# First down pair of each quarter starting with another product, and the weights' sums made in place

## The chip, the cores and the metric

The kernel runs on one core of a Trainium2 chip. The metric is the device time of one execution in microseconds. Before the change it is 960.91 us, the median of three runs (959.47 to 961.05). A profile is one more execution, taken with the hardware profiler.

## The reference, cut to what matters

The program is one decoder block for one sequence of 512 tokens with 1024 channels, in float32: a Mamba-2 mixer and a pooling mixer merged by gates, then an MLP, then a final norm. The change lies in the MLP:

```python
h = rmsnorm(x, norm_mlp_w[i]) * (1.0 + scale_f) + shift_f
x = x + gate_f * (jnp.square(jax.nn.relu(h @ w_up[i])) @ w_down[i])
```

`w_up` is 1024 x 4096 and `w_down` 4096 x 1024.

## The kernel before, in words

**Float32 products.** TensorE is fed numbers of a shorter float format (`fp32r`). A float32 operand is therefore split in two: the high half is a cast on ScalarE (L837, in `two`), the low half is the difference on VectorE, called DVE in the profile (L839). A product is three matmuls: high times high, high times low, low times high. In the plain products these are the lines L156, L157 and L158 (`mm3`), with 512 columns each; in the pairs, all three are L875 (`product`), with 256 columns.

**Quarters.** The 4096 hidden channels are worked on in four quarters q. Within a quarter come the up products (1024 hidden channels, held as eight tiles `us[0]` to `us[7]`, each squared after the ReLU and split), then the down products, which add that quarter's share to x.

**Pairs.** Most of this goes in pairs of 128-wide output tiles, each by seven half-size products of a Strassen-Winograd scheme in place of eight: a 2 x 2 block matrix of weights A11, A12, A21, A22 against a 2 x 2 block matrix of activations B. The weights come with sums formed on the way. `Pair.fetch` loads three tiles: `ya` (1024 wide), `yb` (1024 wide) and `y4` (512 wide). SP issues the three loads (L888, L889, L891), and GpSimd's queue (POOL) then adds further weights onto `ya` and `yb` while loading them (L892, L894). In a pair that is called *led* (the first down pair of each quarter) the second of these adds is made on DVE instead (L911).

From `ya` come the operands S1 and A11 as one split; from the sums z come S2 and S4 as one split; from `yb` come S3 and A12 as one split; `y4` gives A22. The sums are two additions on DVE, 512 wide: the first half of z is the sum of the two halves of `ya` (L908), the second half is the first half of z plus the second half of `yb` (L919). z has a tile of its own.

**The order of a pair.** `run_jobs` writes out the order. Pair after pair it is: A11 times B11 (`first`), the last two products of the pair before (`close` S4, `finish` A22), the preparation of the next pair's `ya` (`prepare`), S2 and then A12 (`middle`), the next pair's sums and its S2/S4 split (`prepare_more`), the next pair's S1 (`open`), S3 (`third`), and then the next pair's S3/A12 and A22 splits (`prepare_rest`). Each product is 4 x 3 = 12 matmuls, so a pair is 84.

The first down pair of a quarter follows a plain down product (`down_plain`, two output tiles), because it needs sums of `us` that are only ready late. Its own preparation is written around that product: `prepare` and `prepare_more` before it, `prepare_rest` behind it. The pair itself then begins with `lead`: A12 times B21 into `c11`, A11 times B11 into `ac`; ScalarE copies `ac` out (L946), DVE adds the copy onto `c11` (L947). It is followed by `open`.

**Slots.** Tiles are given out by `Slots`, first in, first out. RL has four slots for `ya` and `yb`, so two pairs' weights are in flight; a tile that a fetch writes waits until the last reader of its previous content is through. HL has nine slots of 1024 for the high and low halves of split weights; one more tile of that size holds z. The units of `down_plain` take four HL slots, a led pair's S1/A11 and S2/S4 take four.

**What orders the instructions.** The kernel doesn't write the queues out directly: a planner at build time puts the instructions of each engine in a fixed order, from their order in the program, a higher priority where the code says so, and its own estimates of durations. `tc.issue_after(x)` keeps an instruction behind x on x's engine. `mids` holds the DVE additions of the `middle` and `third` products; the sums and some low halves are kept behind the latest of them.

Of the kernel before, what the change touches and what calls it, by code (L numbers as in the profile page):

```python
# [10 lines left out]
ALU = mybir.AluOpType  # L11

P = 128
T = 512
# [26 lines left out]
H = T // 2  # L41
# [21 lines left out]
def block_kernel(tc, xp, crow, arow, par, adaT, wstart, wz, wx, wpool_in, wgate, wpw, wbs, wbp, wout, wup, wdn, out):  # L63
    nc = tc.nc
    act, dve, pool, pe, sp = nc.scalar, nc.vector, nc.gpsimd, nc.tensor, nc.sync

    with (
# [15 lines left out]
        def D(i, dt, o=0):  # L83

            count[0] += 1
            w = 1024 if i < NRAW else 1088
            return sb.tile([P, w], dt, tag=f"d{i}", name=f"d{i}_{count[0]}", bufs=1)[:, o:o + 1024]

        RAW = Slots(D, NRAW)
        HL = Slots(lambda i, dt: D(NRAW + i, dt), NHL)  # L90
        MT = Slots(lambda i, dt: D(NRAW + NHL + i, dt).rearrange("p (h k) -> p h k", h=HG), 3)
# [44 lines left out]
        def load_unit(src, n=1024, low=None, at=None, cols=1024):  # L136

            at = at or HL
            with tc.high_priority() if urgent[0] else nullcontext():
# [76 lines left out]
        def warm(n):  # L216

            ps = PS.get()
            b = busy[:, :T // 2].bitcast(mybir.dt.bfloat16)
            for _ in range(n):  # L220
                pe.matmul(ps, b[:, :P], b, start=True, stop=True)
            PS.put(ps)
# [3 lines left out]
        with tc.manual_schedule():  # L226
# [3 lines left out]
            mt = [MT.get() for _ in range(3)]  # L230
            xs1 = HL.get()
            xpair = [m.rearrange("p h k -> p (h k)") for m in mt] + [xs1]
# [4 lines left out]
            warm(12)  # L237
            wide = HL.get()
            dve.memset(wide, 0.0)
            act.activation(wide[:1], crow_t, AF.Silu)  # L240
            cps = [PU.get(), PU.get()]
            for i in range(2):
                pe.matmul(cps[i], ones, wide[:, i * T:(i + 1) * T], start=True, stop=True)
            HL.put(wide)
            ps = PU.get()
            sq = [HL.get() for _ in range(4)]

# [217 lines left out]
        def ssd_group(g):  # L465
# [20 lines left out]
            def prepare(c):  # L486
# [28 lines left out]
                return m, xdt, xd  # L515

            ready = [prepare(0)]
            yield
            for c in range(NC):
                cc = slice(c * P, (c + 1) * P)  # L520
                if c < NC - 1:
                    ready.append(prepare(c + 1))
                    yield
# [300 lines left out]
        raws = [SZ.get(), SZ.get()]  # L824
        B0 = NRAW
        RL = Slots(lambda i, dt: D(i, dt), 4)
        Z = Slots(lambda i, dt: D(B0 + 8, dt), 1)
        HL = Slots(lambda i, dt: D(B0 + i if i < 8 else B0 + 9, dt, 48), 9)
        HI0 = Slots(lambda i, dt: D(B0 + 10 + i, dt), 2)
        U = Slots(lambda i, dt: slots("pad", 1, (P, T + 16), first=OTHER[i]).get(dt)[:, :T] if i < 2 else spare[i - 2], 4)  # L830
        spare = [S.get(), S.get()]
# [3 lines left out]
        def two(src, dst, late=None):  # L835

            act.copy(dst[0], src)  # L837
            with tc.issue_after(late.ins) if late else nullcontext():
                dve.tensor_tensor(dst[1], src, dst[0].bitcast(F32), ALU.subtract)  # L839
# [37 lines left out]
        class Pair:  # L877
# [25 lines left out]
            def prepare(self):  # L903
                ya = self.y[0]
                self.a, self.left = {}, {}
                z = Z.get()
                with tc.issue_after(mids[-1].ins) if mids and self.led else nullcontext():
                    dve.tensor_tensor(z[:, :T], ya[:, :T], ya[:, T:], ALU.add)  # L908
                if self.led:
                    yb = self.y[1]  # L910
                    dve.tensor_tensor(yb[:, :T], yb[:, :T], ya[:, T:], ALU.add)  # L911
                self.keep(ya, "S1", "A11")
                RL.put(ya)
                self.z = z

            def prepare_more(self):
                z, yb = self.z, self.y[1]
                with tc.issue_after(mids[-1].ins) if mids else nullcontext():
                    dve.tensor_tensor(z[:, T:], z[:, :T], yb[:, T:], ALU.add)  # L919
                self.keep(z, "S2", "S4")  # L920
                Z.put(z)

            def prepare_rest(self):
                yb = self.y[1]
                self.keep(yb, "S3", "A12")
                RL.put(yb)
                hl = Y4S.get(F32R), Y4S.get(F32R)
                two(self.y4, hl)
                Y4S.put(*hl)
                Y4.put(self.y4)  # L930
                self.a["A22"] = hl
# [7 lines left out]
            def lead(self):  # L939
                self.take()  # L940
                self.ac = AC.get()
                self.mul(self.c11, "A12", "B21", True)
                self.mul(self.ac[:, :H], "A11", "B11", True)
                t = U5.get()
                with tc.high_priority():
                    act.copy(t, self.ac[:, :H])  # L946
                    dve.tensor_tensor(self.c11, self.c11, t, ALU.add)  # L947
                U5.put(t)
# [136 lines left out]
        mids = []  # L1085
# [246 lines left out]
```

## Time and profile before

| | |
|---|---|
| median of three runs | 960.91 us |
| lowest, highest | 959.47, 961.05 us |
| the profiled execution | 958.36 us |
| its span | 956.6 us |
| mean granted TensorE clock | 0.995 |
| PE (TensorE matmul) busy | 940.4 us, 98% |
| PEld (its weight loads) busy | 810.9 us, 85% |
| DVE busy | 721.3 us, 75% |
| ACT (ScalarE) busy | 540.8 us, 57% |
| POOL (GpSimd) busy | 124.3 us, 13% |

The span is the time from the first to the last instruction; the difference to the profiled execution's time lies around it. The MLP's pairs take the last 300 us of the span or so. A group row reads: line, engine, operation, output and inputs by the program's names, shape, count, then busy us, mean ns of one, and the engine's idle time just ahead with what ended it. A timeline row begins with the start and the duration in us from the beginning of the span; the brackets at its end hold the idle time before it and what released it. A row of the windows gives the stretch, its length, the busy us of PE, PEld, DVE, ACT and POOL, the granted clock, the DMA share and GB/s. In a row of the chain stand the start, the length and what the time was spent on.

### The profile page before, as it was taken

Reading aid. Unit: us, or ns where it says so; the run is one execution under the profiler, and the core shown is the slowest. Engines: PE = TensorE matmul, PEld = TensorE weight load, DVE = VectorE, ACT = ScalarE, POOL = GpSimd, SP = SyncE. Lnnn points to the kernel's source line nnn. Section 1 sums busy time; section 2 is a strip of 40 time slices with the busy share of each in tenths; the row PEclk is TensorE's granted clock in tenths of the full one; section 3 lists DMA queues with packets and bytes.
Section 4 is the critical chain, followed back from the end, with each engine's and each line's share of the span. In section 5 each row is a group of like instructions: output and inputs, shape, how many; then the busy total and the mean of one; then the engine's idle time right before and its main releaser. Section 6 shows DMA issues by size and latency. Waiting matters only on the chain.

```text
span 956.6 us, 14343 instructions
## 1 busy us (share of the span) xinstructions
PE 940.4 (98%) x5491; PEld 810.9 (85%) x5491; DVE 721.3 (75%) x1120; ACT 540.8 (57%) x891; POOL 124.3 (13%) x131
## 2 busy tenths in 40 slices
PE   8999999999999999999999999999999999999996
PEld 4877888888888888787888888998999899899986
DVE  7978868566767776987568565698869888977973
ACT  5479976568436642553421343486458547646753
POOL 0102320220312031410000000001111111111000
PEclk9999999999999999999999999999999999999998
DMA  9836343433354343464578464035676676677412
GB/s 362 310 119 181 118 129 98 136 121 97 88 144 122 99 116 96 158 192 156 181 237 287 152 201 151 29 91 126 159 200 152 151 198 147 165 194 169 133 35 88
DMA packets 70503, 145.55 MB, mean 152 GB/s; under 512 B 5473, under 2 KB 30305, under 8 KB 70434
## 3 DMA queue, kind: packets, MB, share of 16 engines
q1 hardware_dynamic: 64672, 134.14, 44.5%
q0 software_dynamic: 5760, 10.49, 7.4%
q8 instruction: 43, 0.70, 0.3%
q14 instruction: 26, 0.21, 0.1%
q10 hardware_dynamic: 2, 0.00, 0.0%
HBM read 142.39 MB, written 2.23 MB: 151 GB/s over the span
## 4 chain that ended last, share of the span: by engine, by line
PE 75%; DVE 12%; DMA 5%; ACT 4%; issue 2%; POOL 0%; SPq 0%; DVEq 0%; POOLq 0%; ACTq 0%
PE ps L875 18%; PE ps L156 16%; PE ps L157 16%; PE ps L158 16%; PE ps L328 4%; DMA d<-wdn 3%; DVE d L839 2%; DVE d L147 1%; PE ps L549 1%; DMA d<-cs_d 1%; DVE s L127 1%; DVE s L839 1%; ACT d L837 1%; PE ps L529 1%; DMA d<-wstart 1%
## 5 line engine op out<-in xcount | busy, mean ns | idle before, releaser
L156 PE MATMUL ps<-s,d 128*128 128x512 f32 (+1 forms) x920 | 350.6, 381 | 1.1 <-ACT s L649 0.6
L157 PE MATMUL ps<-s,d 128*128 128x512 f32 (+1 forms) x920 | 345.9, 376 | 0.2 <-DVE s L127 0.2
L158 PE MATMUL ps<-s,d 128*128 128x512 f32 (+1 forms) x920 | 346.0, 376 | 0.0
L156 PEld LDWEIGHTS ps<-s,d 128*128 128x128 f32 x920 | 172.6, 188 | 35.7 <-issue 2.1
L158 PEld LDWEIGHTS ps<-s,d 128*128 128x128 f32 x920 | 172.8, 188 | 32.4 <-issue 0.2
L157 PEld LDWEIGHTS ps<-s,d 128*128 128x128 f32 x920 | 172.8, 188 | 31.2 <-DVE s L127 0.7
L875 PE MATMUL ps<-s,d 128*128 128x256 f32 x1314 | 162.2, 279 | 2.1 <-DVE d L839 2.0
L875 PEld LDWEIGHTS ps<-s,d 128*128 128x128 f32 x1314 | 156.9, 188 | 4.2 <-DVE d L839 3.8
L147 DVE TENSOR_TENSOR d<-d,d 128x1024 fp32r<-128x1024 f32 x88 | 112.6, 1280 | 63.1 <-ACT d L146 56.6
L146 ACT CAST d<-d 128x1024 fp32r<-128x1024 f32 x88 | 92.0, 1046 | 117.8 <-PE ps L157 77.2
L837 ACT CAST d<-d 128x1024 fp32r<-128x1024 f32 x86 | 89.8, 1048 | 56.9 <-DVE d L919 24.1
L839 DVE TENSOR_TENSOR d<-d,d 128x1024 fp32r<-128x1024 f32 x86 | 104.7, 1221 | 18.9 <-ACT d L837 10.2
L172 DVE CUSTOM_DVE_ANT_0 d<-d,d,par_t 128x1024 f32<-128x1024 f32 x32 | 41.8, 1306 | 27.3 <-DMA d<-adaT 27.1
L892 POOL DMA_DIRECT2D d<-wdn x10 | 8.8, 884 | 307.5 <-DMA d<-wdn 258.7
L328 PE MATMUL ps<-s,d 128*128 128x512 f32 x168 | 41.7, 403 | 1.9 <-ACT s L316 1.9
L499 ACT ACTIVATE d<-d,ncs 128x128 f32<-128x128 f32 x128 | 39.9, 390 | 3.9 <-POOL d L495 3.8
L328 PEld LDWEIGHTS ps<-s,d 128*128 128x128 f32 x168 | 32.5, 194 | 10.0 <-ACT s L316 2.4
L397 DVE SCALAR_TENSOR_TENSOR s<-ps,par_t,s 128x511 f32<-128x511 f32 (+2 forms) x54 | 39.6, 741 | 0.3
L126 ACT CAST s<-s 128x512 fp32r<-128x512 f32 x32 | 19.7, 619 | 31.1 <-POOL s L511 18.7
L495 POOL TENSOR_SCALAR_AFFINE_SELECT d<-d 128x1024 f32<-128x1024 f32 x16 | 18.2, 1137 | 90.8 <-ACT cd L492 37.0
L127 DVE TENSOR_TENSOR s<-s,s 128x512 fp32r<-128x512 f32 x32 | 25.7, 805 | 4.4 <-ACT s L126 4.3
L511 POOL TENSOR_TENSOR s<-s,dec 128x512 f32<-128x512 f32 x12 | 15.8, 1313 | 90.7 <-issue 56.4
(231 smaller groups left out, 1231.6 us busy)
## 6 DMA issues: line engine op xcount, KB each, us to landing
d<-adaT SPq DMA_DIRECT2D x32, 512.0 KB, 4.2
d<-wup SPq DMA_DIRECT2D x32, 512.0 KB, 4.8
d<-wdn SPq DMA_DIRECT2D x32, 512.0 KB, 4.6
d<-wx SPq DMA_DIRECT2D x18, 512.0 KB, 3.6
d<-cs_d SPq DMA_DIRECT2D x16, 512.0 KB, 6.0
d<-wbs SPq DMA_DIRECT2D x16, 512.0 KB, 3.6
d<-wgate SPq DMA_DIRECT2D x16, 512.0 KB, 4.2
d<-wz SPq DMA_DIRECT2D x15, 512.0 KB, 3.6
```

The costliest lines, as they stand in the source:

```text
L146: act.copy(hi[:, :w], r[:, a:a + w])
L147: (low or dve).tensor_tensor(lo[:, :w], r[:, a:a + w], hi[:, :w].bitcast(F32), ALU.subtract)
L156: pe.matmul(ps, whi, xhi[:, t0:t1], start=start, stop=False)
L157: pe.matmul(ps, whi, xlo[:, t0:t1], start=False, stop=False)
L158: pe.matmul(ps, wlo, xhi[:, t0:t1], start=False, stop=stop)
L172: dve.tensor_tensor_reduce(r, r, cbc, 1.0, col("b_ada", j), ALU.mult, ALU.add, mod[:, j:j + 1])
L328: pe.matmul(first[u], w[u][i // 2], h[k][i % 2], start=k == 0 and i == 0, stop=k == 7 and i == 2)
L397: dve.scalar_tensor_tensor(t[:, sh:], ps[:, :T - sh], w(3 - sh), t[:, sh:], ALU.mult, ALU.add)
L499: act.activation(m[:, i, :], m[:, i, :], AF.Exp, bias=ncs[:, c, g * HG + i:g * HG + i + 1])
L837: act.copy(dst[0], src)
L839: dve.tensor_tensor(dst[1], src, dst[0].bitcast(F32), ALU.subtract)
L875: pe.matmul(ps, x, y, start=start and m == 0 and i == 0, stop=m == 3 and i == 2, skip_group_check=True)
```

## The change

Four edits in the pairs of the MLP.

1. `lead`, the beginning of the first down pair of each quarter, makes A11 times B11 first and A12 times B21 second. Before, it was the other way round.
2. The sums have no tile of their own any more. The first is written over the first half of `ya`, after the S1/A11 split has read it; the second over the second half of `ya`. `ya` is given back after the S2/S4 split, not after the S1/A11 split. The first sum of a led pair is no longer kept behind `mids`.
3. The tile that z had becomes the tenth HL slot, for split weights.
4. The S3/A12 split moves from `prepare_rest` to the end of `prepare_more`: ahead of the next pair's S1 and this pair's S3 product in the program, and for a led pair ahead of the plain down product.

```diff
--- before.py
+++ after.py
@@ -824,8 +824,7 @@
         raws = [SZ.get(), SZ.get()]
         B0 = NRAW
         RL = Slots(lambda i, dt: D(i, dt), 4)
-        Z = Slots(lambda i, dt: D(B0 + 8, dt), 1)
-        HL = Slots(lambda i, dt: D(B0 + i if i < 8 else B0 + 9, dt, 48), 9)
+        HL = Slots(lambda i, dt: D(B0 + i, dt, 48), 10)
         HI0 = Slots(lambda i, dt: D(B0 + 10 + i, dt), 2)
         U = Slots(lambda i, dt: slots("pad", 1, (P, T + 16), first=OTHER[i]).get(dt)[:, :T] if i < 2 else spare[i - 2], 4)
         spare = [S.get(), S.get()]
@@ -903,27 +902,22 @@
             def prepare(self):
                 ya = self.y[0]
                 self.a, self.left = {}, {}
-                z = Z.get()
-                with tc.issue_after(mids[-1].ins) if mids and self.led else nullcontext():
-                    dve.tensor_tensor(z[:, :T], ya[:, :T], ya[:, T:], ALU.add)
                 if self.led:
                     yb = self.y[1]
                     dve.tensor_tensor(yb[:, :T], yb[:, :T], ya[:, T:], ALU.add)
                 self.keep(ya, "S1", "A11")
+                dve.tensor_tensor(ya[:, :T], ya[:, :T], ya[:, T:], ALU.add)
+
+            def prepare_more(self):
+                ya, yb = self.y
+                with tc.issue_after(mids[-1].ins) if mids else nullcontext():
+                    dve.tensor_tensor(ya[:, T:], ya[:, :T], yb[:, T:], ALU.add)
+                self.keep(ya, "S2", "S4")
                 RL.put(ya)
-                self.z = z
-
-            def prepare_more(self):
-                z, yb = self.z, self.y[1]
-                with tc.issue_after(mids[-1].ins) if mids else nullcontext():
-                    dve.tensor_tensor(z[:, T:], z[:, :T], yb[:, T:], ALU.add)
-                self.keep(z, "S2", "S4")
-                Z.put(z)
-
-            def prepare_rest(self):
-                yb = self.y[1]
                 self.keep(yb, "S3", "A12")
                 RL.put(yb)
+
+            def prepare_rest(self):
                 hl = Y4S.get(F32R), Y4S.get(F32R)
                 two(self.y4, hl)
                 Y4S.put(*hl)
@@ -939,8 +933,8 @@
             def lead(self):
                 self.take()
                 self.ac = AC.get()
+                self.mul(self.ac[:, :H], "A11", "B11", True)
                 self.mul(self.c11, "A12", "B21", True)
-                self.mul(self.ac[:, :H], "A11", "B11", True)
                 t = U5.get()
                 with tc.high_priority():
                     act.copy(t, self.ac[:, :H])
```

## The prediction

> **What bounds the kernel now.** I read the page first, then the waits of TensorE, then the timeline of the MLP stage engine by engine. Page, parts 1 and 5:
>
> ```profile
> span 956.6 us, 14343 instructions
> ...
> PE 940.4 (98%) x5491; PEld 810.9 (85%) x5491; DVE 721.3 (75%) x1120; ACT 540.8 (57%) x891; POOL 124.3 (13%) x131
> ...
> L875 PE MATMUL ps<-s,d 128*128 128x256 f32 x1314 | 162.2, 279 | 2.1 <-DVE d L839 2.0
> L875 PEld LDWEIGHTS ps<-s,d 128*128 128x128 f32 x1314 | 156.9, 188 | 4.2 <-DVE d L839 3.8
> ```
>
> TensorE is the bound. In the products of the pairs (L875) its only wait that sums to anything is for L839 on DVE, the low half of a split of weights: 2.0 us as idle PE, 3.8 us as idle weight loads. The timeline of the weight loads shows where:
>
> ```profile
> 673.07 2.65 PEld L875 LDWEIGHTS ps<-s,d 128*128 128x128 f32 x22 [0.74 <-DVE d L839]
> 737.20 3.95 PEld L875 LDWEIGHTS ps<-s,d 128*128 128x128 f32 x33 [0.35 <-DVE d L839]
> 754.28 2.65 PEld L875 LDWEIGHTS ps<-s,d 128*128 128x128 f32 x22 [0.60 <-DVE d L839]
> 818.42 3.93 PEld L875 LDWEIGHTS ps<-s,d 128*128 128x128 f32 x34 [0.36 <-DVE d L839]
> 835.25 2.57 PEld L875 LDWEIGHTS ps<-s,d 128*128 128x128 f32 x22 [0.49 <-DVE d L839]
> 897.58 2.54 PEld L875 LDWEIGHTS ps<-s,d 128*128 128x128 f32 x21 [0.94 <-DVE d L839]
> 914.43 2.65 PEld L875 LDWEIGHTS ps<-s,d 128*128 128x128 f32 x22 [0.36 <-DVE d L839]
> ```
>
> Seven waits, 3.84 us together. By the order of the products, 673, 754, 835 and 914 are the first product of the four led pairs, A12 times B21 (0.74 + 0.60 + 0.49 + 0.36 = 2.19 us). The other three, 737, 818 and 898, are A12 times B21 in the last up pair of a quarter, just ahead of the plain down product (`down_plain`, L1180) (0.35 + 0.36 + 0.94 = 1.65 us). All seven wait for the low half of A12. Why it is late in the second quarter, from DVE, ScalarE, the queues and PE:
>
> ```profile
> 726.79 0.34 SPq L888 DMA_DIRECT2D d<-wdn  x1
> 730.65 1.22 DVE L839 TENSOR_TENSOR d<-d,d 128x1024 fp32r<-128x1024 f32 x1
> 734.79 2.35 DVE L839 TENSOR_TENSOR d<-d,d 128x1024 fp32r<-128x1024 f32 x2
> 736.04 1.05 ACT L837 CAST d<-d 128x1024 fp32r<-128x1024 f32 x1 [1.32 <-DMA d<-wdn]
> 737.00 0.62 ACT L1093 ACTIVATE pad<-pad 128x512 f32<-128x512 f32 x1
> 741.37 0.62 ACT L837 CAST d<-pad 128x512 fp32r<-128x512 f32 x1 [0.92 <-DVE pad L844]
> 743.08 0.62 ACT L837 CAST d<-pad 128x512 fp32r<-128x512 f32 x1 [0.81 <-DVE pad L846]
> 744.77 1.22 DVE L839 TENSOR_TENSOR d<-d,d 128x1024 fp32r<-128x1024 f32 x1
> 749.79 1.02 DVE L839 TENSOR_TENSOR s<-s,s 128x512 fp32r<-128x512 f32 x2
> 751.66 0.39 PE L157 MATMUL ps<-s,d 128*128 128x512 f32 x1
> 753.01 1.22 DVE L839 TENSOR_TENSOR d<-d,d 128x1024 fp32r<-128x1024 f32 x1
> ```
>
> The row at 753.01 is A12's low half; it ends at 754.23 and PE resumes at 754.28. DVE has no idle time before it: its place in DVE's order makes it late, and that place comes from the slots. Of nine slots for split weights the down product's two units hold four and the led pair's S1/A11 and S2/S4 four, so the second tile of S3/A12 is one that the first unit gives back at the end of the down product. A11's low half was done at 744.77 + 1.22 = 745.99, more than seven us before its turn. At 734.79 the second of two rows is A12's low half of the last up pair, behind those of the down product's own units.
>
> **The change part by part.** Instruction and DMA counts stay. The sums change their tile:
>
> ```profile
> L908 DVE TENSOR_TENSOR d<-d x22: 678/690/695, 652.8 to 903.5; 128x512 f32<-128x512 f32 x22
> L911 DVE TENSOR_TENSOR d<-d,d x4: 683/684/685, 654.3 to 904.1; 128x512 f32<-128x512 f32 x4
> ```
>
> L911 already sums in place and takes 684 ns against 690 for L908: zero, at most 22 x 6 ns either way.
>
> *A11 first in the led pair.* A11 is split in time in all four quarters if its row keeps its place, and the product is 12 matmuls, half of the 24 that take about 2.65 us at 754.28, so 1.3 to 1.4 us of cover. The longest led wait is 0.74. This edit alone takes the 2.19 us even if the split of A12 doesn't move. The add of L947 needs both products as before.
>
> *Tenth slot and sooner split.* S3/A12 is now taken with S2/S4, before the down product, and ten slots are just enough (4 + 6), so no tile has to come back from the units. In the pairs that follow each other the third operand no longer waits for the product of the one before. This takes the 1.65 us ahead of the down products. What remains is whether DVE has room. Removed: upper bound 3.84; lower bound 2.0, the idle of PE itself from the page; I take 3.5, nearer the upper, since weight loads and matmuls alternate one by one here and a late load is a late product.
>
> *What is late next.* S3/A12's low half (1.22 us) now ranks before the splits of the last activated tile, us[7]. That is the first of the two rows at 749.79 (half of a merged row, some 0.69 us long, so done at 750.48); PE reads it at 751.66: 1.18 us to spare. In the first quarter there is less:
>
> ```profile
> 669.15 1.03 DVE L839 TENSOR_TENSOR s<-s,s 128x512 fp32r<-128x512 f32 x2
> 670.30 0.39 PE L157 MATMUL ps<-s,d 128*128 128x512 f32 x1
> ```
>
> Done at about 669.85, read at 670.30: 0.45 us. Pushed by 1.22: 0.04 us in later quarters and 0.77 in the first; from the latter the first sum of the next pair (L908, 0.69) is to be taken off, since it now stands behind that pair's own split. Bounds 0 and 1.1 us, I take 0.5.
>
> *The first weight tile is held longer.* It was free after the low half of S1/A11; now after that of S2/S4, because the sums live in it. The refill is one SP load and one POOL add, in this order on both queues. Among the up pairs:
>
> ```profile
> 692.88 1.22 DVE L839 TENSOR_TENSOR d<-d,d 128x1024 fp32r<-128x1024 f32 x1
> 694.13 0.34 SPq L888 DMA_DIRECT2D d<-wup  x1
> 699.30 1.23 DVE L839 TENSOR_TENSOR d<-d,d 128x1024 fp32r<-128x1024 f32 x1 [0.24 <-ACT d L837]
> 700.41 0.86 POOL L892 DMA_DIRECT2D d<-wup  x1 [0.38 <-issue]
> 711.29 1.05 ACT L837 CAST d<-d 128x1024 fp32r<-128x1024 f32 x1 [0.98 <-PE ps L875]
> 712.71 0.36 ACT L968 COPY ps<-ps 128x256 f32<-128x256 f32 x1 [0.36 <-PE ps L875]
> 715.34 8.64 PE L875 MATMUL ps<-s,d 128*128 128x256 f32 x72
> ...
> d<-wup POOLq DMA_DIRECT2D x24, 256.0 KB, 4.3
> ```
>
> (The last row is from the page's DMA issues.) The load at 694.13 goes right behind the low half that ends at 694.10. It will go behind the one that ends at 700.53, 6.4 us later. Its tile was whole at about 700.41 + 4.3 + 0.9 = 705.6 (the 0.9 being the issue itself) and cast at 711.29, when a slot came free from PE: 5.7 us of cover. So the cast comes some 0.7 us later, 712.0, and its low half ends by about 714.4. The products of the row at 715.34 are S2 and A12 of the pair before, 24 matmuls at 0.118, and then S1, which reads it at about 718.2: nothing lost, while the loads take no longer. Behind the cast on ScalarE stands L968, whose copy must be out before that S2 at 715.34; it ends at 713.07 and has 2.3 us. The second tile (L889, L894) is freed sooner and costs nothing. Taken as 0, bounds -0.2 and +2 us for the whole stage.
>
> **Sum.** -3.5 + 0.5 + 0 = -3.0 us. The profiled execution took 958.36 (span 956.6 and 1.76 around it), 2.55 below the median 960.91 of the three runs shown. So 955.4 for a run like it, and 957.9 against the median.
>
> **The rivals.**
>
> *The split moves, the wait moves with it.* If both halves of S3/A12 are put ahead of us[7], 1.05 us on ScalarE joins the 1.22: 2.27 - 1.18 = 1.09 us in three quarters and 1.82 in the first, 5.1 us. -3.5 + 5.1 = +1.6, 962.5. For it: DVE is nearly full there.
>
> ```profile
> 720.00:760.00 40.00, 39.57 (x288) 37.10 (x288) 36.03 (x60) 27.92 (x50) 4.33 (x5) 1.00 0.66 164
> ```
>
> 36.03 of 40 us on DVE (fourth number after the colon; PE 39.57). Against: the total doesn't grow and ScalarE, at 27.92, has room for the cast anywhere.
>
> *Slower: a cast that waits for a late tile holds ScalarE.* At 736.04 the cast of the led pair's S1/A11 had already held ScalarE for 1.32 us, waiting for its weights. Their load (726.79) went behind S1/A11 of the up pair before; it will go behind the low half that ends at 730.65 + 1.22 = 731.87, 5.1 us later, so the tile is whole at 741.2. If the cast keeps its place ahead of L1093, the whole chain of us[6] and us[7] starts 5.1 us late. ScalarE's idle rows of 0.92 and 0.81 give back at most 1.7, us[7] has 1.18 to spare: 2.2 to 3.9 us in each of three quarters (the first quarter's led weights come in slots that plain units held). 6.6 to 11.7, say 9; with the -3.5 it is 966.4. It decides from a tile more than 1.2 us behind its place. Against: the written order is made knowing the later load, so the cast should move down, and S1/A11 has over seven us before its use.
> The Trainium skill, "TensorE: Matmul & The Clock Gate", section "Architectural detail: the array is 16× 32×32, not 1× 128×128", speaks for this one: ScalarE's and VectorE's queues are strict FIFO, only TensorE pulls anything forward. The 1.32 us at 736.04, with work right behind it, agrees.
>
> *Half of it.* The planner leaves A12's low half last on DVE. Then the three waits ahead of the down products stay: -2.19, 958.7.
>
> *The pace of PE.* The chain of waits has three long runs of products:
>
> ```profile
> 673.07 50.93 PE ps L875 x430
> ...
> 754.28 50.93 PE ps L875 x430
> ...
> 835.25 57.06 PE ps L875 x501
> ```
>
> 118.4, 118.4 and 113.9 ns a product, the same instructions at the same granted clock (1.00). The pace differs from one restart after a wait to the next, and the change removes the restarts. If the third run falls to the slow pace, 501 x 4.5 ns = 2.3 us are lost: 960.2. If the first two rise, 2 x 430 x 4.5 ns = 3.9 us are won: 954.0. Nothing in the trace says which; the forecast leaves each run its pace.
>
> **How the numbers follow.** Forecast (956.8 to 959.1, from -3.84 with nothing given back to -2.0 with little) 0.48; half 0.12; the wait moves 0.14; pace lost 0.08; pace won 0.06; ScalarE held 0.12. A measurement of this kernel tells about 0.2%, 1.9 us, from no change: faster is below 959.0. Faster: most of the forecast, half of the half, the pace won, 0.55. Slower, above 962.8: ScalarE held and a tail of the moved wait, 0.14. Within: 0.31. The range 954.4 to 962.4 takes in all but the held ScalarE and the edges of the moved wait and the won pace.
>
> **What would show it.** Right: no wait for L839 at the first product of a led pair, nor in the last up pair of a quarter, idle weight loads there below 1 us together; A12's low half before us[7]'s or soon after, and ahead of the sums of u; SP's first load of a pair behind S2/S4. Wrong: new waits of L156 to L158 for an s tile of L839 in the down product (the wait moved); ScalarE idle for several us on a weight load ahead of L1093 (held); the L875 runs at another mean per product (pace).

## The result and the profile after

The changed kernel takes 968.5 us, the median of four runs (967.32 to 972.54). The kernel before, run beside it, takes 960.25. The ratio is 1.0106, with a 95% interval of 1.0085 to 1.0127: 1.1% slower, and outside the predicted range. The profiled execution took 968.73 us, its span is 967.0.

Lines have moved: the cast of a split is now L836 (before L837), the low half L838 (L839), a pair's products L874 (L875), the loads of `ya` and `yb` L887 and L888, the first sum L909, the second L914, the DVE add of a led pair's `yb` L907, the DVE sum of `middle` L967 (L973), the ReLU of the up products L1086 (L1092). From the page of the changed kernel:

```profile
PE 945.4 (98%) x5491; PEld 813.2 (84%) x5491; DVE 719.8 (74%) x1120; ACT 540.3 (56%) x891; POOL 124.7 (13%) x131
...
L874 PE MATMUL ps<-s,d 128*128 128x256 f32 x1314 | 162.3, 279 | 1.2 <-DVE ps L967 1.2
L874 PEld LDWEIGHTS ps<-s,d 128*128 128x128 f32 x1314 | 157.8, 188 | 2.2 <-DVE ps L967 1.7
```

The wait for the low half of A12 is gone from both groups: where 2.0 and 3.8 us stood under L839, the releaser is now L967. The busy times of DVE and ScalarE are the same as before within 1.5 us, so no work was added. The same is seen in the waits of the whole changed kernel (engine, what it works on, what it waited for; us in total, times, longest):

```profile
PE ps L874 <- DVE ps L967: 2.4, 5, 0.9
...
PE ps L156 <- ACT pad L1086: 1.4, 1, 1.4
...
PE ps L156 <- ACT s L836: 1.3, 2, 1.1
...
PE ps L157 <- DVE s L838: 1.0, 3, 0.4
```

None of these four rows is in the view of before. They sum to 6.1 us of idle PE. TensorE now waits for the middle sums of pairs (L967; two of the five waits stand in the last up pair of a quarter, three in down pairs) and, in the plain products (L156, L157), for activated tiles.

What is late ahead of them? The same view between 622 and 945 us, for the weights alone (`wup` and `wdn` are the sources in memory). Changed kernel:

```profile
ACT d L836 <- DMA d<-wup: 13.4, 5, 3.6
ACT d L836 <- DMA d<-wdn: 11.4, 3, 4.3
DVE d L907 <- DMA d<-wdn: 3.2, 2, 2.8
```

Kernel before:

```profile
DVE d L908 <- DMA d<-wdn: 4.6, 1, 4.6
...
ACT d L837 <- DMA d<-wdn: 3.9, 3, 1.5
```

ScalarE's casts of weights stood waiting for loads for 24.8 us, against 3.9 before. How such a wait gets to TensorE shows in the second quarter. ScalarE, changed kernel, with the tile's loads from SP's queue and the products that come too late:

```profile
736.70 1.79 SPq L887 DMA_DIRECT2D d<-wdn  x2
742.29 0.62 ACT L836 CAST s<-pad 128x512 fp32r<-128x512 f32 x1
746.78 1.05 ACT L836 CAST d<-d 128x1024 fp32r<-128x1024 f32 x1 [3.87 <-DMA d<-wdn]
747.74 0.38 ACT L1086 ACTIVATE s<-ps 128x256 f32<-128x256 f32 x1
754.06 1.05 ACT L836 CAST d<-d 128x1024 fp32r<-128x1024 f32 x1 [1.35 <-DVE d L914]
755.02 0.63 ACT L1087 ACTIVATE s<-s 128x512 f32<-128x512 f32 x1
756.52 0.49 PE L156 MATMUL ps<-s,d 128*128 128x512 f32 x1 [0.17 <-ACT s L836]
757.36 0.50 PE L157 MATMUL ps<-s,d 128*128 128x512 f32 x1 [0.35 <-DVE s L838]
```

The row at 746.78 is the cast of the led pair's S1/A11. It held ScalarE for 3.87 us (1.32 before); its load was issued at 736.70 (726.79 before; PE's products around it stand some 3.9 us later as well, so about 6 us of this are the tile's). Behind it stands the ReLU of us[6] (L1086), and then comes us[7]. The cast of S2/S4 (754.06) stands ahead of us[7]'s square as it did before, and waited 1.35 us for the second sum on DVE (0.37 before). The square (755.02) ends at 755.65, and its split comes when TensorE already needs it. The middle sums hang on late tiles too, at least in one case: in the down pair where PE waits at 703.41, DVE's work was held by a cast that had waited 3.47 us for its weights (ScalarE, 697.19).

Not all of the difference of the two profiles is the change's. Counting PE's instructions from the start, the 3000th begins at 617.87 us before and at 620.00 after, ahead of all work that the change touches. The other 8.3 us arise behind it. There PE's waits, taken as what each start-to-start time has above the usual 0.118 or 0.2285 us, sum to 10.5 us against 4.7. The third long run of products has lost its fast pace, some 2.3 us, but others have won it: counted over all pairs, 282 products ran at the fast pace against 581 before, some 1.3 us lost. The last 1.1 us were not taken apart.

### The profile page after: what moved, and what is told of

Its sections match the earlier page's. It is cut to its first block, busy times and chain, and to the rows that moved or that the text cites. A ratio compares the mean times of both kernels' runs of the same rounds, so it can differ in the third digit from the quotient of the medians.

```text
span 967.0 us, 14359 instructions
## 1 busy us (share of the span) xinstructions
PE 945.4 (98%) x5491; PEld 813.2 (84%) x5491; DVE 719.8 (74%) x1120; ACT 540.3 (56%) x891; POOL 124.7 (13%) x131
## 4 chain that ended last, share of the span: by engine, by line
PE 68%; DVE 15%; DMA 7%; ACT 5%; issue 4%; POOL 0%; SPq 0%; DVEq 0%; ACTq 0%; POOLq 0%
PE ps L156 16%; PE ps L157 16%; PE ps L158 16%; PE ps L874 12%; PE ps L328 4%; DMA d<-wdn 4%; DVE d L838 2%; DMA d<-cs_d 2%; DVE d L147 2%; ACT d L836 1%; DVE s L127 1%; PE ps L549 1%; DMA d<-wup 1%; DVE s L838 1%; DVE pad L631 1%
## 5 line engine op out<-in xcount | busy, mean ns | idle before, releaser
L156 PE MATMUL ps<-s,d 128*128 128x512 f32 (+1 forms) x920 | 351.1, 382 | 4.2 <-ACT pad L1086 1.4
L157 PE MATMUL ps<-s,d 128*128 128x512 f32 (+1 forms) x920 | 346.7, 377 | 1.3 <-DVE s L838 1.0
L156 PEld LDWEIGHTS ps<-s,d 128*128 128x128 f32 x920 | 172.6, 188 | 40.7 <-ACT s L836 2.5
L157 PEld LDWEIGHTS ps<-s,d 128*128 128x128 f32 x920 | 172.8, 188 | 33.0 <-DVE s L838 2.0
L874 PE MATMUL ps<-s,d 128*128 128x256 f32 x1314 | 162.3, 279 | 1.2 <-DVE ps L967 1.2
L874 PEld LDWEIGHTS ps<-s,d 128*128 128x128 f32 x1314 | 157.8, 188 | 2.2 <-DVE ps L967 1.7
L836 ACT CAST d<-d 128x1024 fp32r<-128x1024 f32 x86 | 89.6, 1049 | 85.5 <-DVE d L914 26.2
L838 DVE TENSOR_TENSOR d<-d,d 128x1024 fp32r<-128x1024 f32 x86 | 104.7, 1222 | 43.4 <-ACT d L836 37.2
L874 PE MATMUL ps<-sz,d 128*128 128x256 f32 x180 | 26.7, 283 | 1.1 <-DVE ps L967 1.1
```

The lines of the kernel that those rows point to most:

```text
L156: pe.matmul(ps, whi, xhi[:, t0:t1], start=start, stop=False)
L157: pe.matmul(ps, whi, xlo[:, t0:t1], start=False, stop=False)
L874: pe.matmul(ps, x, y, start=start and m == 0 and i == 0, stop=m == 3 and i == 2, skip_group_check=True)
```

## The experiments

In the expectations, "traced" means written in the program; the planner makes the queues from it.

### The order of the led pair alone

```
 (kernel before)
             def lead(self):
-                self.mul(self.c11, "A12", "B21", True)
                 self.mul(self.ac[:, :H], "A11", "B11", True)
+                self.mul(self.c11, "A12", "B21", True)
```

> The kernel before with one edit: each led pair's product of block 11 (A11) is traced ahead of A12's, nothing else. Theory (the first weight tile, held longer, is what costs the 8 us): this edit doesn't touch that tile, so the four waits of led pairs for A12's low half (2.19 us in all in the profile of before) go, the three of the last up pairs (1.65 us) stay, and the time is 957.5 to 958.5. Rival (the led pair's new order itself is harmful, as A11's unit is needed one product, about 1.4 us, sooner): new waits for A11's low half stand where the old ones stood, and the time is 960 to 964.

Measured: 955.5 us beside 959.81, ratio 0.9957 (0.9943 to 0.9971). Faster, and by more than the 2.19 us of the waits; the interval of the gain is 2.8 to 5.5 us. The rival falls. In the profile the chain of waits shows that pace helped here:

```profile
673.95 63.63 PE ps L875 x538
...
754.25 31.30 PE ps L875 x276
...
834.08 57.02 PE ps L875 x503
```

118.3, 113.4 and 113.4 ns a product (length over count): the second of these ran at the fast pace too. Counted from start to start, 1087 of the pairs' products ran at it, against 581 in the first profile of the kernel before; at 4.5 ns each this is 2.3 us, as much as the two profiled executions differ (956.14 and 958.36). PE's waits in the pairs fell by only 0.9 us, since the waits of the last up pairs for A12 grew. So how much of the 4.3 us belongs to the order is not settled.

### The sums in place alone, and the tile held alone

```
 (kernel before, first experiment)
-        z = Z.get(); first sum: z[:, :T] = ya[:, :T] + ya[:, T:]
         self.keep(ya, "S1", "A11")
-        RL.put(ya)
+        first sum: ya[:, :T] = ya[:, :T] + ya[:, T:]
 ...
-        second sum into z; self.keep(z, "S2", "S4"); Z.put(z)
+        second sum into ya; self.keep(ya, "S2", "S4"); RL.put(ya)
```

> The kernel before with the sums alone put in place in the first weight tile, which is so freed behind the split of S2/S4 and not behind that of S1/A11; nine split slots, A12 split where it was, A12's product first. Theory (the tile's refill starts later, and the casts that need it hold ScalarE): the seven waits for A12 stay (3.8 us), and most of the 8 us of the change is there: 964 to 968; ScalarE's casts of pairs wait for the weight load. Rival (the sooner split of S3/A12 puts work ahead of nearer work on DVE and ScalarE, the tile is harmless): 960 to 961.

```
 (kernel before, second experiment)
         self.keep(ya, "S1", "A11")
-        RL.put(ya)
 ...
         self.keep(z, "S2", "S4")
+        dve.tensor_tensor(z[:, :8], z[:, :8], ya[:, :8], ALU.add)
         Z.put(z)
+        RL.put(ya)
```

> The kernel before with one edit: the first weight tile is freed only behind the split of S2/S4. An addition of eight columns on DVE reads it there and holds it (its result goes into a tile that is no longer read, so that what is computed is the same; it costs some 0.1 us per pair on DVE). Sums, slots, order and split stay as before. Theory (held tile): ScalarE's casts of S1/A11 wait for the load as in the change, and the time is 964 to 969, like the kernel with the sums in place. Rival (what costs is in the sums in place or in the sooner split, not the tile's holding): 960 to 962.

Measured: sums in place 970.16 us beside 959.81, 1.0115 (1.0088 to 1.0141); tile held 979.26, 1.0209 (1.0186 to 1.0232). Both are slower than the theory had them (964 to 968, 964 to 969). Holding the tile is enough to make the kernel slower, with sums, order and splits as before (the 22 additions that hold it take 0.16 us each on DVE). One reason why it costs even more than the change is in the same view, weights alone, between 622 and 945 us:

```profile
ACT d L837 <- DMA d<-wdn: 16.6, 3, 7.3
DVE d L908 <- DMA d<-wdn: 11.7, 4, 4.1
DVE d L908 <- DMA d<-wup: 7.8, 5, 2.4
ACT d L837 <- DMA d<-wup: 7.7, 3, 2.7
DVE d L911 <- DMA d<-wdn: 6.1, 3, 4.6
```

Here the first sum (L908) still goes ahead of the split, so that DVE stands waiting for the late tile as well. PE waits at the same place as in the change, longer (kernel with the tile held):

```profile
PE ps L156 <- ACT s L837: 8.0, 3, 4.4
```

With the sums in place alone this is 5.0 us, also in three waits: the plain down product waits for us[7] once in each of three quarters. The rivals that blame the sums or the sooner split fall.

A second reason is TensorE's clock. Behind the longest of these waits (4.6 and 3.1 us from start to start) the granted clock fell to 0.50 for about 6.8 us, twice: at half the clock, that is up to some 6.8 us lost on top of the waits. The same happens, for about 3.4 us at a time, in several of the kernels below. The profiles of the kernel before and of the change have no such stretch between 640 and 935 us, so it is no part of their difference.

### Sums in the second tile

```
 (kernel after)
         self.keep(ya, "S1", "A11")
-        ya[:, :T] = ya[:, :T] + ya[:, T:]
 ...
+        self.keep(yb, "S3", "A12")
+        yb[:, :T] = ya[:, :T] + ya[:, T:]
+        RL.put(ya)
-        ya[:, T:] = ya[:, :T] + yb[:, T:]; self.keep(ya, "S2", "S4"); RL.put(ya)
-        self.keep(yb, "S3", "A12"); RL.put(yb)
+        yb[:, T:] = yb[:, :T] + yb[:, T:]; self.keep(yb, "S2", "S4"); RL.put(yb)
```

> The kernel after, except that the two sums are written into the second weight tile: S3/A12 is split first, then the first sum goes over it and the first tile is freed, then the second sum and the split of S2/S4. Sooner split, ten split slots and A11 first stay as in the change; the first tile is freed about one split of ScalarE (1.2 us) later than before, the second one later still. Theory (held first tile): the refill of the first tile starts some 4 us sooner than in the change, the cast waits for it shrink, and the time is 957 to 962. Rival (the sooner split, or the order of the two tiles' refills, whichever tile is late): the waits go over to the second tile, 965 to 969.

Measured: 969.25 us, 1.0103 (1.0065 to 1.0142). My theory as I had put it fell; the rival was right. The waits for weights between 622 and 945 us:

```profile
ACT d L836 <- DMA d<-wup: 12.7, 8, 2.9
DVE d L907 <- DMA d<-wdn: 9.0, 4, 2.4
```

The second tile is the late one now, and another instruction waits for it, the led pair's add on DVE (L907). PE waits 6.8 us for L967, behind it on DVE. Holding either of the two tiles costs about the same.

### The first order with the sooner split kept

```
 (kernel after)
             def lead(self):
-                self.mul(self.ac[:, :H], "A11", "B11", True)
                 self.mul(self.c11, "A12", "B21", True)
+                self.mul(self.ac[:, :H], "A11", "B11", True)
```

> The kernel after with one edit: each led pair begins with A12's product again, as before the change. Sums in place, ten split slots and the sooner split stay. Against the sums alone (970.2 us) it shows what the sooner split of S3/A12 brings, against the kernel after (968.5) what the order of the led pair brings once A12 is split sooner. Theory (A12 is early enough since the sooner split, so that the order is worth nothing there): 968 to 969. Rival (A12's waits come back in the led pairs): 969.5 to 971.

Measured: 968.06 us beside 959.46, 1.0090 (1.0075 to 1.0105). As the theory had it: with A12 split sooner the order is worth nothing. Against the sums in place alone (1.0115) the sooner split may have brought some 2 us, but the two intervals overlap.

### A12 split sooner without a held tile

```
 (kernel before with A11 first)
+            def keep_half(self, y, n, o):
+                t = HL.get(F32R)
+                hl = t[:, :T], t[:, T:]
+                two(y[:, o:o + T], hl)
+                self.a[n], self.left[n] = hl, (t,)
 ... prepare_more, behind the split of S2/S4
+                self.keep_half(yb, "A12", T)
 ... prepare_rest
-                self.keep(yb, "S3", "A12")
+                self.keep_half(yb, "S3", 0)
```

> The kernel before with A11's product first in led pairs (which ran 955.5 us alone) and with A12's half of the second weight tile split by itself, as early as the change splits it: its two parts lie side by side in the ninth split slot, S3's two in one slot later. The sums stay in their own tile and the first tile is freed as before. The second tile's split so takes two casts of 512 columns (0.61 us each) and two subtractions (0.69 us) for one of 1.05 and one of 1.22, 0.17 and 0.16 us more for each pair. Theory (the sooner split is good, only the held tile was bad): the waits left in the last up pairs (1.3 and 0.8 us) go and nothing comes in their place: 953 to 954.5. Rival (the sooner split costs, as its work stands ahead of nearer sums on ScalarE and DVE): waits of the up pairs for DVE's sums, 956 to 959.

Measured: 961.31 us, 1.0022 (1.0010 to 1.0034). The waits for A12 in the last up pairs are gone, but the kernel is slower than with A11 first alone (0.9957). DVE and PE in the second quarter:

```profile
733.85 0.69 DVE L917 TENSOR_TENSOR d<-d,d 128x512 f32<-128x512 f32 x1
736.65 0.69 DVE L839 TENSOR_TENSOR s<-pad,s 128x512 fp32r<-128x512 f32 x1 [2.11 <-ACT s L837]
737.26 0.43 DVE L980 TENSOR_TENSOR ps<-ps,pad 128x256 f32<-128x256 f32 x1
737.74 1.52 PE L875 MATMUL ps<-s,d 128*128 128x256 f32 x11 [1.44 <-DVE ps L980]
```

The middle sum of the last up pair (L980) stands behind a low half of us[4] that waits for ScalarE (its cast there comes behind the led pair's, which waited 1.46 us for its weights, 1.32 before the change); PE lost 3.4 us so in three quarters. The rival's waits are there, and the time is above its range (956 to 959): the sooner split is not free, even with the first tile freed as before. Two half-size splits also take some 0.3 us more for each pair on ScalarE and DVE together; what that costs was not separated.

### The led pair's cast moved behind us[7]

```
 (in two, activated and keep; on the kernel after, then on the sums in place alone)
-            act.copy(dst[0], src)
+            cast = act.copy(dst[0], src)
 ...
+            return cast
 ...
-            two(u, us[2 * p + i])
+            casts.append(two(u, us[2 * p + i]))
 ...
+            with tc.issue_after(casts[-1].ins) if mids and self.led else nullcontext():
                 two(y, hl, mids[-1] if mids and self.led else None)
 ... run_jobs, ahead of a led pair: prepare and prepare_more traced behind last.finish()
```

> The kernel after, with the led pair's preparation in quarters 2 to 4 traced behind the last up pair's last product, and its casts on ScalarE ordered behind the cast of us[7]; the tile comes as late as in the change. Theory (it is the late tile's cast, standing at the head of ScalarE, that delays us[7]): the waits of the plain down product for us[7] (1.0, 2.0 and 0.8 us, with the restarts behind them) go, and some of this comes back as a wait of the led pair for A11; the waits of the up pairs for DVE's sums (2.4 us) and quarter 1's (1.7 us) stay: 964.5 to 966.5. Rival (the order on ScalarE is not the cause): 968 to 969.5, with us[7] as late as before.

> The kernel with the sums in place alone (970.2 us; its waits are in the plain down product, for us[7], 5.0 us and the restarts behind them), with the led pair's preparation in quarters 2 to 4 traced behind the last up pair's last product and its casts on ScalarE ordered behind the cast of us[7]. There the sooner split is absent. Theory (the late tile costs only as long as its cast stands at the head of ScalarE): the waits for us[7] go and 961 to 964 is left. Rival (as in the same reordering of the changed kernel, the led pair's split comes later still, and the wait comes back in the pairs behind it): 967 to 971, with waits of L875 for ScalarE's first copy or for splits in the pairs after the led one.

Measured: on the kernel after 970.43 us beside 959.46, 1.0112 (1.0095 to 1.0129); on the sums in place 967.78 beside 957.78, 1.0112 (1.0082 to 1.0143). Both times the waits for us[7] went and both times the time stayed: the rival's result in the second run. In the first the time is above the rival's 968 to 969.5, and its condition, us[7] as late as before, did not hold. In the kernel after, they came back in the pairs behind the led one, 6.0 us for ScalarE's first copy in three waits. In the other, this is what stood at the head of DVE, and what PE waited for:

```profile
742.75 0.69 DVE L910 TENSOR_TENSOR d<-d,d 128x512 f32<-128x512 f32 x1 [2.84 <-DMA d<-wdn]
...
754.48 3.54 PE L876 MATMUL ps<-s,d 128*128 128x256 f32 x17 [1.98 <-DVE d L839]
```

The cast was out of the way on ScalarE, but the led pair's add onto `yb` (L910 here), which reads the same tile, waited in its place on DVE. The led pair's splits also came later by the edit itself. So these two runs did not yet tell a late tile from a badly placed instruction.

### Which pairs' tiles matter

```
 (kernel before; a pair with hold keeps its sums in ya, as in the sums in place;
  a pair without it has z as before)
+            pair = Pair(wup[4 * q + p], ...)
+            pair.hold = p == 3          # first kernel: all others without
+            pair.hold = p < 3           # second kernel: all others with
```

> The kernel before with the sums in place, and so the first tile held, in the last up pair of quarters 2 to 4 alone: three pairs. All other pairs keep their own tile for the sums. The last up pair's first tile is the one that the led pair's first tile is loaded into. Theory (the loss is the led pair's late first tile): nearly the whole loss of the sums in place is there, 966 to 970, with waits of the plain down product for us[7]. Rival (every held tile costs a little): 961 to 963.

> The counterpart: the sums in place in all pairs except the last up pair of quarters 2 to 4, where they keep their own tile and the first weight tile comes free as before. Theory (the loss is the led pair's late first tile): 958.5 to 961, as before the change, with no wait for us[7]. Rival (every held tile costs a little): 966 to 970.

Measured: three pairs held 969.51 us, 1.0130 (1.0093 to 1.0167); all but these three held 970.89, 1.0159 (1.0123 to 1.0196), both beside 957.78. The first is as the theory had it: three tiles carry the whole loss, with 5.7 us of waits for us[7]. Behind each of these three waits the granted clock fell to 0.50 for about 3.4 us, up to another 5.1 us in this profile. The first time (the clock is the third number from the end):

```profile
754.00:757.00 3.00, 2.88 (x7) 1.94 (x7) 3.00 (x8) 1.87 (x4) 0.86 (x1) 0.50 0.41 91
```

The second run is not as the theory had it: no wait for us[7], yet as slow, by one wait of 2.5 to 3.2 us in the second up pair of quarters 2 to 4, each again with about 3.4 us at half the clock behind it. There the last up pair's first sum, which still went into z, headed DVE, ahead of that pair's middle sum, and waited up to 6.6 us for its tile. Two runs moved it:

```
 (second kernel; first edit)
-        if z is not None: z[:, :T] = ya[:, :T] + ya[:, T:]      # ahead of the split
         self.keep(ya, "S1", "A11")
+        if z is not None: z[:, :T] = ya[:, :T] + ya[:, T:]; RL.put(ya)
 (second edit, in place of the first: prepare_more)
+        if not self.hold:
+            with tc.issue_after(mids[-1].ins):
+                z[:, :T] = ya[:, :T] + ya[:, T:]
+            RL.put(ya)
```

> The counterpart once more (sums in place in all pairs but the last up pair of quarters 2 to 4, whose first tile comes free early), with one edit: in that pair the first sum, which goes into its own tile, is traced behind the split of S1/A11 and not ahead of it. In the run before this one that sum stood at the head of DVE and waited up to 6.6 us for its late tile; PE waited 3.3, 2.6 and 3.3 us for the DVE work behind it. Theory (a tile that comes late costs only where an instruction waiting for it heads the queue of an engine with nearer work behind it): those three waits go and 959 to 962 is left. Rival (the held tiles cost by themselves, as too little time is left for the refills): 967 to 971, with the waits elsewhere in the up pairs.

> The counterpart a third time: sums in place in all pairs but the last up pair of quarters 2 to 4. Tracing that pair's first sum behind its split did not move it: it stood at the head of DVE again and waited 6.1 us for its tile. Here it is taken together with the second sum and ordered behind the middle sum of the pair before, so that on DVE it stands behind the low half of S1/A11 (18 places later). Theory (a late tile costs only where an instruction that waits for it heads an engine's queue ahead of nearer work): PE's three waits of 2 to 3 us for DVE's middle sum (L975) go, no wait for us[7] comes back, and the time is 959 to 963. Rival (too little time is left for the refills of held tiles, whatever the order): 967 to 971, with waits for splits of the last up pairs and the led pairs instead.

Measured: 972.41 us beside 957.71, 1.0143 (1.0103 to 1.0184), and 961.03 beside 958.57, 1.0022 (1.0009 to 1.0035). The first edit changed nothing in DVE's order, since the sum doesn't need the split. DVE and PE in that kernel:

```profile
719.67 0.69 DVE L914 TENSOR_TENSOR d<-d 128x512 f32<-128x512 f32 x1 [6.11 <-DMA d<-wup]
720.28 0.68 DVE L839 TENSOR_TENSOR s<-pad,s 128x512 fp32r<-128x512 f32 x1
720.88 0.42 DVE L975 TENSOR_TENSOR ps<-ps,pad 128x256 f32<-128x256 f32 x1
721.36 1.86 PE L875 MATMUL ps<-s,d 128*128 128x256 f32 x14 [2.67 <-DVE ps L975]
```

The same place with the second edit:

```profile
717.67 0.69 DVE L839 TENSOR_TENSOR s<-pad,s 128x512 fp32r<-128x512 f32 x1 [2.40 <-ACT s L837]
718.28 0.42 DVE L977 TENSOR_TENSOR ps<-ps,pad 128x256 f32<-128x256 f32 x1
...
728.84 0.68 DVE L920 TENSOR_TENSOR d<-d 128x512 f32<-128x512 f32 x1
```

The sum (L914, now L920) no longer waits; the middle sum is done before PE needs it. One addition moved in three pairs takes the slowdown from 1.4% to 0.2%, with the sums in place everywhere else and those tiles held. In its profile PE's only waits left in the pairs are three of 1.0 us for L839, at the led pairs. So among the up pairs a late tile costs where an instruction that waits for it stands ahead of nearer work on its engine, and held tiles cost little otherwise. For the led pair's first tile, the one that the change makes late, this is seen in the trace (the 3.87 us at 746.78) but not shown by an edit: the last kernel frees that tile sooner, and the two runs with the cast moved stayed as slow.

### What the gain would have been

> The run before this one (961.0 us: sums in place except in the last up pair of quarters 2 to 4, whose first sum stands behind the split), with the led pair's A11 product first as in the change. Its profile has three waits of 1.2 us left, for A12's low half at the first product of led pairs. Theory (the order of the led pair takes its waits away whatever the tiles do, since nothing late heads a queue any more): 3 to 3.6 us less, 957 to 958.5. Rival (the order brings nothing beside held tiles, as between the two kernels with the sooner split, 968.1 and 968.5): 960.5 to 961.5.

The edit is that of the first experiment, made on the last kernel. Measured: 958.32 us beside 958.27, 1.0006 (0.9994 to 1.0018), against 1.0022: about 1.5 us of gain, though the two intervals overlap. The time lies in the theory's range and the led pairs' three waits are gone, but the gain is half of what was expected, and waits of 0.8 us for A12 in a last up pair and of 0.6 us for a middle sum have come. ScalarE still stood 20.4 us for weights there, but never longer than 2.3:

```profile
ACT d L837 <- DMA d<-wup: 12.5, 8, 1.9
ACT d L837 <- DMA d<-wdn: 7.9, 4, 2.3
```

So the sum of such waits says little; what stands behind each decides.

```
 (kernel before with A11 first; last up pair of quarters 2 to 4 only)
-        z[:, :T] = ya[:, :T] + ya[:, T:]          # prepare
 ... prepare_more, in front of the second sum
+        z[:, :T] = ya[:, :T] + ya[:, T:]; RL.put(ya)
```

> No tile held: the kernel before with A11 first in the led pairs (955.5 us alone), and the first sum of the last up pair of quarters 2 to 4 taken together with its second sum. That first tile is freed behind the sum and not sooner. In the run with the same sum placed so, the waits of the last up pairs for A12 were gone; in the kernel with A11 first alone they are 1.3, 0.8 and 0.2 us. Theory (these waits hang on what stands ahead of A12's low half on DVE, and the first sum is one of these): they go, 953.5 to 955. Rival (they come from the tile's release or the pace): 955 to 957.

Measured: 960.12 us, 1.0024 (1.0013 to 1.0034): slower than either had it. The last up pairs' waits for A12 went, but waits of 0.7 us at led pairs came instead. Why they came is open. In the two profiles PE's waits don't explain the difference to A11 first alone; the pace does: here no product of the pairs ran at the fast pace, there 1087 did, 4.9 us at 4.5 ns each, where the profiled executions differ by 3.5 us. Whether the edit or the execution decides that is open as well. No version tried beats A11 first alone, at 955.5 us.

### The kernel before, profiled again

> The kernel before, unchanged, profiled a second time. The first 150 us of the changed kernel's profile, where no line differs, were 2.06 us longer than here, and its third long run of products kept the pace of 117.8 ns where the profile of before shows 113.3. Theory (both differ from one execution to the next): PE's position at 600 us is off by 0.5 us or more from the first profile, or the stretches at 113.3 ns stand elsewhere. Rival (both belong to the program): the two profiles agree within 0.2 us there and in where the fast pace stands.

It took 958.8 us. PE's instructions in the first 150 us, from the windows of the first and this profile (third in the row: PE, with its count):

```profile
0.00:150.00 150.00, 144.42 (x678) 110.70 (x679) 120.22 (x194) 111.74 (x193) 28.10 (x35) 0.99 0.59 198
```

```profile
0.00:150.00 150.00, 144.08 (x683) 110.41 (x684) 121.40 (x196) 112.94 (x194) 28.21 (x35) 1.00 0.61 198
```

It is five instructions ahead, and its 3000th begins 1.0 us sooner; over all kernels here, which share the lines up to there, it begins from 2.5 us sooner to 2.1 later. And from its chain:

```profile
834.57 63.87 PE ps L875 x540
```

118.3 ns a product, where the first profile of the same kernel had 113.9. Both differences belong to the execution, not to the change.

## Why the prediction was wrong, point by point

**A12's waits vanish: right.** All seven are gone, and both ways predicted for it work: the order of the led pair alone, and the sooner split alone. As a size, the led pair's order brought 4.3 us (2.8 to 5.5) where 2.19 were counted; in the profiled execution the gain is pace, which also changes between executions of one kernel.

**"The first weight tile is held longer ... Taken as 0, bounds -0.2 and +2": the step that failed.** It measured some 10 to 12 us: the sums in place alone, which hold the tile in all pairs, added 10.4 us, and holding it in three pairs 11.7; holding it with the sums left where they were added 19.5 (2.1%). The step compared the tile's lateness with the cast's own reader in one up pair and found cover. For the led pair it did this only in a rival, and it asked too little what stands behind each waiting instruction. The 3.5 us that the sum took off for A12 did come off; this term outweighed them.

**"The cast should move down": the argument that failed in the rival.** The slower rival had the mechanism and one of its places, and got a chance of 0.12 because the planner was thought to know the later load. The cast did move down, but not far enough. The L1093 at 737.00, ahead of which it stood before, is the square of us[4], not of us[6] as the rival has it; after the change it stands behind the splits of us[4] and us[5], and still ahead of the ReLU of us[6]. That the rival's time came near (966.4 against 968.5) is luck: it had 6.6 to 11.7 us of waits for us[6] and us[7], and the profile shows 2.3 us for us[7], with the rest at middle sums, in quarter 1 and in the pace. The planner also put first sums at DVE's head where they waited 6 us, and writing one of them later in the program changed nothing. The Trainium skill, "TensorE: Matmul & The Clock Gate", section "Architectural detail: the array is 16× 32×32, not 1× 128×128", has ScalarE and VectorE as strict FIFO queues. These traces agree: in the 3.87 us at 746.78 ScalarE did nothing, though us[6]'s ReLU stood right behind.

**"S3/A12's low half now ranks before the splits of us[7]", 0.5 us: wrong place.** us[7] was late first by ScalarE's waiting cast: with the sums in place alone, where A12 is split as late as before, it is waited for longer (5.0 us). DVE's 1.22 us may add to it in the change, as it stands ahead of the second sum for which ScalarE waited 1.35 us; that was not separated. The sooner split does have a cost at another place, the middle sum of the last up pair: 3.4 us of waits in the run without held tiles, which the prediction did not list.

**The second tile, "freed sooner and costs nothing": not contradicted.** What stays open is quarter 1: the wait of 1.4 us (ACT pad L1086) comes while DVE's add L907, which reads both tiles, waits 2.8 us for a load of `wdn`. A like wait of PE is in the profiles of the four kernels with ten split slots and in none of the others, so it goes with these; it was not taken apart.

**Pace: right that it can be lost; that the change loses it is not shown.** The unchanged kernel lost it as well.

## What to carry to other kernels

When a buffer is freed later, don't ask only whether its own reader has time: find every instruction that will wait for the refill, on each engine, and read what is queued behind it. A planner with estimated durations need not move a waiting instruction far enough out of the way, as here; an explicit edge behind the nearer work did so for one addition, and for a cast it moved the wait to a second reader of the same tile, so look for that reader too. Try the parts of a change one by one: here one swapped line was worth 0.4%, and the rest of the change turned it into a loss of 1.1%.

## What was not expected of the hardware

The same products run at one of two paces at the same granted clock (1.00): about 113.3 or 117.8 ns from start to start for a product of 256 columns, for tens of us at a time (113.4 and 118.3 where a whole run's length is divided by its count). The unchanged kernel's third run of products had 113.9 in one execution and 118.3 in another. Over 500 products the two paces differ by some 2.3 us, as much as many edits here. What sets the pace was not found. And the first 620 us, with the same instructions, differ by up to 4.6 us between profiled executions.

A wait of TensorE can also cost more than its length. Behind waits of 1.6 to 4.6 us the granted clock fell to 0.50 for about 3.4 us or twice that, which loses up to 1.7 us or twice that again. It did not always: the kernel with the first edit of "Which pairs' tiles matter" has three waits of 2.3 to 2.9 us and no such stretch. What decides it was not found.
